# A hybrid RWKV-7/pooling decoder step: an account of array use that holds back steps of tiny products, a VectorE transpose in place of 32-wide products, and idle products in the first norm

## The chip, the cores and the metric

One NeuronCore of a Trainium2 chip runs the whole step. Its engines work side by side: TensorE (PE, with its weight loads PEld), VectorE (DVE), ScalarE (ACT), GpSimd (POOL), and the DMA queues, most of them issued from SyncE (SP). The metric is the device time of one execution in microseconds; a comparison uses medians over several runs.

## The reference

The reference is one inference step of a one-layer decoder trunk of width 1024 for a prompt of 1024 tokens and eight samples of 8 tokens, 1088 columns in all, in float32:

- `h = RMSNorm(x)`, scaled and shifted per request by a conditioning vector (the factors come from a small product with `w_ada_mix`).
- `P = h @ w_in`, 34 blocks of 128 output columns: 14 for RWKV-7, 4 for pooling, 16 for the gates.
- RWKV-7 branch: token shift, a data-dependent decay, and a recurrence over time for each of 8 heads of 64. The kernel computes it in chunks of 64 tokens, which needs the inverse of a 64x64 unit triangular matrix for each chunk, then a group norm.
- pooling branch: means over 2, 4, 8 and 16 tokens and a 128x128 product for each group.
- both branches are multiplied into the trunk through `w_br`, gated, then `w_out`, then a second norm and an MLP (`w_ff1`, squared ReLU, `w_ff2`), then a last norm.

## The kernel before

All tensors lie with features on the 128 partitions and the 1088 tokens along the free axis, in three chunks of 364, 362 and 362 (`CH`). Every large product is done as three FP32R products, high part times high, high times low, low times high (`mm3`), into PSUM.

**Order of TensorE's work.** TensorE's instructions run in the order in which they are recorded; the other engines are ordered by the framework's scheduler. `Pace.run` writes that order. It has one stream in the background (`back`: the large products of `w_in`, `w_br`, later `w_out` and the MLP; one `yield` after each three products of a chunk) and some generators in the foreground (`fore`: the chunked recurrence, pooling, norms). A foreground generator yields either a delay in modelled nanoseconds or a condition; it continues when `Pace.t`, the modelled time, has passed that delay, or the condition holds. Until then background products are recorded. `K.mm` and `K.tr` add each product's modelled duration to `Pace.t`; a change of array shape (32, 64 or 128 rows and columns) adds 200 ns. If the background yields "idle" too, `Pace.t` jumps to the earliest delay.

**Phase 1** has `start` (the first norm), then `heads` (the four head pairs f = 0 to 3 in turn), `chains` (the serial recurrence, 64x64 products), `pools` and `or_rows` in the foreground, and the `w_in` and pooling half of `w_br` products behind them. For each f, `heads` runs `front`, `scores`, then `main` (`inverse`, `level`, `affine`) beside `post` of the head pair before it; for f = 0 the neighbour is a conditioning product. `both` interleaves two such generators. Phase 2 starts with the RWKV half of `w_br` (`or_job`), which reads the result of the last `post`.

**level** finishes the triangular inverse, 32x32 blocks at a time, 16 chunks x 4 groups: a first step of 64 products, a second step of 64 products `nd` x `zd` into `ps` and 32 products `zd` x `nd` into `px` (the same blocks transposed, wanted as `x32` by the third step), then a third and a fourth step of 32 products. ACT copies `ps` into `z` with four instructions (L863), VectorE copies `px` into `x32` with two (L859). `ps` and `px` are buffers of the PSUM tag "w", which has 2; "wc" has 2 and "mm" has 4.

**rinv** (in `front` and in `post`'s `norm`) sums squares over a head with up to nine 128x128 products of 2 columns each, then ACT and VectorE make the inverse root, and `spread` transposes it back on TensorE.

**start** squares the eight blocks of x on ACT, sums them on TensorE with a matrix of ones, and then, for four groups of two feature blocks (qi = 0 to 3), computes the conditioning factors: two rounds of 32-column products (`round_`, weights `aw` by DMA), a copy to `asb` on ACT (L410), a small product `pv` (`vectors`), then the rows of h, high and low parts (`rows`, L432 to L435). The first `w_in` products run beside it as rows become ready.

## Time and profile before

| what | value |
|---|---|
| median of the three runs shown | 1767.05 us (1756.51 to 3532.46) |
| the profiled execution, whole | 1762.42 us |
| its span, first to last instruction | 1760.6 us |
| PE busy / DVE / ACT / POOL | 1702.3 / 843.5 / 549.6 / 281.9 us |
| mean granted TensorE clock over the span | 0.980 |

The page of the profile says how long each engine was busy, in which slices, at which granted clock (PEclk, in tenths), which chain of work ended last, and which groups of instructions cost most. Almost all products are recorded by the helper at L148 and are told apart by the tiles they read and write: `mm<-hx,whi` is a large product, `w<-iv,hv` and `w<-hv,iv` are the two halves of `level`'s second step, `w<-kct,wt` of 2 columns is `rinv`. One fp32 product is two instructions, one FP32R product is one.

### The profile page before, as it was taken

The numbers are of one execution on the slowest core, as the hardware profiler recorded it, in microseconds if no ns is written. First come the engines' busy times: TensorE is split into PE (matmuls) and PEld (weight loads), VectorE is DVE, ScalarE is ACT, GpSimd is POOL, SyncE is SP. The second block draws the span as 40 slices with busy tenths as digits, with TensorE's granted clock in tenths as the row PEclk, the third lists the DMA queues.
The fourth block names the chain that finished last, engine by engine and source line by source line (L and its number), as shares of the span: only waits on it lengthen the run. The fifth ranks groups of instructions, "written<-read, shape, count | busy, mean of one in ns | idle before, by whom it ended". The sixth has DMA issues, their size and how long they took to land.

```text
span 1760.6 us, 32648 instructions
## 1 busy us (share of the span) xinstructions
PE 1702.3 (97%) x13712; PEld 1590.2 (90%) x13712; DVE 843.5 (48%) x1554; ACT 549.6 (31%) x1108; POOL 281.9 (16%) x379
## 2 busy tenths in 40 slices
PE   5999999999999999999999999999999999999997
PEld 3989878887888798889889999999999999999997
DVE  5576466736583744344436633433333333333255
ACT  4443333434343433222225521313121222212132
POOL 3310101100000000004414511110111111111121
PEclk8999999989999999999999999999999999999999
DMA  9233314222413241857852321111111111111112
GB/s 335 74 124 130 124 64 136 80 82 79 162 46 128 71 139 61 292 181 258 295 176 79 125 68 43 44 47 43 48 43 43 49 43 42 48 43 43 48 43 102
DMA packets 80787, 179.61 MB, mean 102 GB/s; under 512 B 11360, under 2 KB 25696, under 8 KB 80640
## 3 DMA queue, kind: packets, MB, share of 16 engines
q1 hardware_dynamic: 72960, 155.63, 26.1%
q10 hardware_dynamic: 6048, 16.23, 2.8%
q0 software_dynamic: 1632, 5.67, 1.0%
q8 instruction: 108, 1.77, 0.4%
q14 instruction: 39, 0.32, 0.1%
HBM read 138.64 MB, written 38.84 MB: 101 GB/s over the span
## 4 chain that ended last, share of the span: by engine, by line
PE 87%; DVE 5%; DMA 3%; ACT 2%; issue 2%; POOL 1%; SPq 0%; DVEq 0%; ACTq 0%; POOLq 0%
PE mm L148 58%; PE w L148 24%; PE wc L148 4%; DMA t<-d_th 1%; PE w L155 1%; POOL t L1318 1%; DMA x<-in_xT 1%; DVE t L1377 0%; DVE wlo L168 0%; DMA hid<-in_w_ada_mlp 0%; DVE ma L1379 0%; DVE h L432 0%; DVE bk L664 0%; DVE d L496 0%; DVE t L1486 0%
## 5 line engine op out<-in xcount | busy, mean ns | idle before, releaser
L148 PE MATMUL mm<-hx,whi 128*128 128x362 f32 (+2 forms) x2608 | 683.3, 344 | 2.5 <-ACT px L517 2.0
L148 PEld LDWEIGHTS mm<-hx,whi 128*128 128x128 f32 x2608 | 459.0, 191 | 39.8 <-issue 19.2
L148 PE MATMUL mm<-hx,wlo 128*128 128x362 f32 (+3 forms) x1304 | 430.6, 330 | 0.3 <-DVE wlo L168 0.3
L167 ACT ACTIVATE whi<-wraw 128x512 fp32r<-128x512 f32 x246 | 155.1, 630 | 538.9 <-PE w L148 362.2
L148 PE MATMUL mm<-ma,whi 128*128 128x364 f32 (+1 forms) x1280 | 319.3, 330 | 0.3 <-DVE ma L1322 0.3
L148 PEld LDWEIGHTS mm<-hx,wlo 128*128 128x128 f32 x1304 | 249.8, 192 | 0.7 <-DVE wlo L168 0.6
L148 PEld LDWEIGHTS mm<-ma,whi 128*128 128x128 f32 x1280 | 227.5, 189 | 8.2 <-issue 7.5
L168 POOL TENSOR_TENSOR wlo<-wraw,whi 128x512 fp32r<-128x512 f32 x91 | 119.0, 1309 | 676.0 <-ACT whi L167 672.4
L148 PE MATMUL mm<-ma,wlo 128*128 128x364 f32 (+1 forms) x640 | 210.8, 329 | 0.2 <-DVE wlo L168 0.2
L168 DVE TENSOR_TENSOR wlo<-wraw,whi 128x512 fp32r<-128x512 f32 x155 | 108.8, 702 | 208.6 <-ACT whi L167 208.3
L1526 DVE SCALAR_TENSOR_TENSOR hx<-mm,aq,hx 128x364 f32<-128x364 f32 (+3 forms) x136 | 75.0, 588 | 206.2 <-PE mm L148 206.1
L148 PE MATMUL w<-mb,whi 128*128 128x362 f32 x576 | 143.8, 331 | 0.0
L148 PEld LDWEIGHTS mm<-ma,wlo 128*128 128x128 f32 x640 | 121.1, 189 | 0.5 <-DVE wlo L168 0.5
L1401 DVE TENSOR_TENSOR ft<-ft 128x362 f32<-128x362 f32 (+1 forms) x96 | 53.1, 576 | 131.4 <-ACT ft L1400 131.1
L148 PEld LDWEIGHTS w<-mb,whi 128*128 128x128 f32 x576 | 102.6, 191 | 2.5 <-issue 1.7
L148 PE MATMUL w<-hx,whi 128*128 128x362 f32 x416 | 103.5, 330 | 0.0
L148 PE MATMUL w<-mb,wlo 128*128 128x362 f32 x288 | 95.5, 332 | 1.8 <-DVE wlo L168 1.8
L148 PEld LDWEIGHTS w<-hx,whi 128*128 128x128 f32 x416 | 73.7, 190 | 1.7 <-issue 1.7
L148 PE MATMUL mm<-hid,whi 128*128 128x364 f32 (+4 forms) x304 | 74.9, 328 | 0.0
L1400 ACT ACTIVATE ft<-mm 128x364 f32<-128x364 f32 x64 | 29.5, 475 | 125.6 <-PE mm L148 125.5
L148 PE MATMUL w<-hx,wlo 128*128 128x362 f32 x208 | 67.8, 326 | 0.0
L1531 POOL TENSOR_TENSOR hx<-hx,rs 128x64 f32<-128x64 f32 x72 | 39.2, 544 | 142.1 <-DVE rs L1529 142.1
(330 smaller groups left out, 2196.8 us busy)
## 6 DMA issues: line engine op xcount, KB each, us to landing
wraw<-in_w_ff SPq DMA_DIRECT2D x134, 256.0 KB, 2.6
wraw<-in_w_in SPq DMA_DIRECT2D x68, 256.0 KB, 2.8
hid<-in_w_ada_mlp SPq DMA_DIRECT2D x24, 512.0 KB, 4.5
d_th<-px SPq DMA_DIRECT2D x22, 544.0 KB, 3.1
wt<-d_x SPq DMA_DIRECT2D x20, 544.0 KB, 4.3
t<-d_th ACTq DMA_DIRECT2D x16, 544.0 KB, 5.5
aw<-in_w_ada_mix SPq DMA_DIRECT2D x16, 512.0 KB, 9.2
wraw<-in_w_out SPq DMA_DIRECT2D x32, 256.0 KB, 2.7
```

The source lines that it names most:

```text
L148: return self.nc.tensor.matmul(out, lhsT, rhs, **kw)
L155: self.nc.tensor.transpose(out, in_, ident)
L167: nc.scalar.activation(hi, raw, AF.Copy)
L168: (nc.gpsimd if n < 2 or n % 2 and n >= self.solo else nc.vector).tensor_tensor(lo, raw, hi.bitcast(F32), op=ALU.subtract)
L1318: nc.gpsimd.tensor_tensor(t, t, S["u"], op=ALU.add)
L1400: nc.scalar.activation(t[:, :n], ps[:, :n], AF.Relu)
L1401: nc.vector.tensor_tensor(t[:, :n], t[:, :n], t[:, :n], op=ALU.mult)
L1526: nc.vector.scalar_tensor_tensor(x[:, c0:c0 + m], ps[:, :m], gt[:, 0:1], x[:, c0:c0 + m], op0=ALU.mult, op1=ALU.add)
L1531: nc.gpsimd.tensor_tensor(x[:, NPR:NT], x[:, NPR:NT], t, op=ALU.add)
```

## The change

`Pace` gets an account: each product adds its modelled time times a share that says how much of the array it uses (1 for FP32R, less for narrow fp32 products, 0 for fewer than 16 columns, 0.5 for transposes). `Pace.warm(t)` is a condition that a foreground step can yield in place of a delay t: the delay must have passed, and, while the background has products to give, the account over the last 3400 ns must be over `WARM` = 1700. It stands before `rinv` in `front` and in `norm`, and before all four steps of `level`; 25 times in all. When both are idle, `Pace.t` advances by 100 ns; `both` hands up one condition in place of a computed delay. In `level` the 32 products into `px` and their copies go, and VectorE transposes `ps` in 32x32 blocks into `x32`; the delay before the third step is 3000 in place of 4000. In `start`, one product of ones with x (128x128, 512 columns, never read) is put before `pv` of qi = 0, and two before the first round of qi = 1; the delays between `asb` and `pv` grow from 1100 to 1800, and to 2600 for qi = 1.

```diff
+    def spend(self, t, share):
+        self.t += t
+        self.work.append((self.t, t * share))
+
+    def warm(self, t):
+        end = self.t + t
+        def ready():
+            while self.work and self.work[0][0] < self.t - 3400:
+                self.work.pop(0)
+            return self.t >= end and (not self.dense or sum(w for _, w in self.work) > WARM)
+        return ready
...
+                self.dense = r != "idle"
                 if r == "idle" and live:
-                    self.t = max(self.t, min(r for r in live.values() if not callable(r)))
+                    self.t += 100
...
-        self.pace.t += n / 2.4 + 14 if rhs.dtype == F32R else max(n / 0.6 * min(mode) / 128, 30) + 3
+        if rhs.dtype == F32R:
+            self.pace.spend(n / 2.4 + 14, 1)
+        else:
+            self.pace.spend(max(n / 0.6 * min(mode) / 128, 30) + 3, 0 if n < 16 else max(mode) / 128 if min(mode) > 32 else 0.1)
...
-        self.pace.t += 2 * math.prod(ident.shape[1:]) / 2.4 + 3
+        self.pace.spend(2 * math.prod(ident.shape[1:]) / 2.4 + 3, 0.5)
...
+        def spin(po, n):
+            for _ in range(n):
+                self.mm(po, ones, xs[0][:, 0:512], start=True, stop=True)
...
                 ps[qi] = self.ps("wc")
+                spin(ps[qi], 2 if qi == 1 else 0)
...
             pv = self.ps("wc")
+            spin(pv, 1 if qi == 0 else 0)
...
-                yield from vectors(qi, 1100)
+                yield from vectors(qi, 2600 if qi == 1 else 1800)
...
-        yield 8000 if f else 11000
+        yield self.pace.warm(8000 if f else 11000)
...
-        yield 5500
+        yield self.pace.warm(5500)
...
-        yield 3000
-        ps, px = self.ps("w"), self.ps("w")
+        yield self.pace.warm(3000)
+        ps = self.ps("w")
...
-        for c in range(16):
-            for g in G[::2]:
-                self.mm(at(px, g, c), zd[g, c, :], nd[g, c, :], **tp(g))
-        x32 = cut32(self.hv())
-        for g in G[::2]:
-            nc.vector.tensor_copy(x32[g], cut32(px)[g])
+        x32 = self.hv()
+        nc.vector.transpose(x32, ps)
+        x32 = cut32(x32)
...
-        yield 4000
+        yield self.pace.warm(3000)
...
-        yield 3000
+        yield self.pace.warm(3000)
...
-            yield 2500 if last else 5000
+            yield self.pace.warm(2500 if last else 5000)
...
-            ready = [x for x in live if (x[1]() if callable(x[1]) else x[1] <= pace.t)]
+            now = lambda: [x for x in live if (x[1]() if callable(x[1]) else x[1] <= pace.t)]
+            ready = now()
             if not ready:
-                times = [x[1] for x in live if not callable(x[1])]
-                yield (min(times) - pace.t) if times else 500
+                yield lambda: bool(now())
...
+WARM = 1700
```

More of the change, by code (lines that the diff above doesn't have):

```diff
@@ L85, in __init__ @@
         self.t = 0.0
+        self.work = []
+        self.dense = False
+    def spend(self, t, share):
[8 more added lines that the diff above has]
+        return ready
     def run(self, back, fore=(), until=lambda: False):
```

## The prediction

> **What bounds the kernel now.** I read the page first: busy times, the slices with the granted clock, the chain that ended last.

> ```profile
> span 1760.6 us, 32648 instructions
> PE 1702.3 (97%) x13712; PEld 1590.2 (90%) x13712; DVE 843.5 (48%) x1554; ACT 549.6 (31%) x1108; POOL 281.9 (16%) x379
> PEclk8999999989999999999999999999999999999999
> PE 87%; DVE 5%; DMA 3%; ACT 2%; issue 2%; POOL 1%; SPq 0%; DVEq 0%; ACTq 0%; POOLq 0%
> ```

> TensorE is busy 97% of the span and is 87% of the chain that ended last. So every microsecond of TensorE time before the end counts, and other engines count only where TensorE waits for them. What can still go is its idle time (1760.6 − 1702.3 = 58 us), products that need not be, and time at a lower clock. The clock line has rounded digits, so I next asked for stretches cut where the clock changes (PE, PEld, DVE, ACT, POOL busy, then the granted clock).

> ```profile
> 354.34:357.75 3.41, 1.53 (x152) 1.42 (x141) 0.00 (x0) 2.17 (x4) 0.00 (x0) 1.00 0.03 6
> 576.21:579.62 3.41, 3.41 (x33) 3.12 (x32) 2.59 (x7) 2.19 (x3) 0.00 (x0) 1.00 0.00 0
> 30.07:43.73 13.66, 10.73 (x42) 7.38 (x42) 11.84 (x20) 5.26 (x9) 8.82 (x14) 0.50 1.08 349
> 245.11:248.53 3.42, 3.42 (x19) 2.82 (x18) 0.28 (x1) 1.03 (x3) 0.00 (x0) 0.50 0.09 27
> 357.75:367.99 10.24, 9.57 (x73) 9.51 (x74) 1.76 (x4) 3.72 (x7) 0.00 (x0) 0.50 0.01 2
> 422.61:429.43 6.82, 6.82 (x80) 5.43 (x80) 6.75 (x12) 1.85 (x4) 0.00 (x0) 0.50 0.14 42
> 525.01:531.83 6.82, 6.82 (x27) 6.29 (x27) 0.86 (x2) 3.09 (x6) 0.00 (x0) 0.50 0.01 2
> 542.07:545.48 3.41, 3.41 (x32) 3.35 (x25) 1.42 (x3) 2.29 (x3) 0.00 (x0) 0.50 0.28 97
> 579.62:583.03 3.41, 3.41 (x19) 3.01 (x17) 0.25 (x1) 1.35 (x3) 0.00 (x0) 0.50 0.24 77
> 692.26:699.09 6.83, 6.83 (x28) 6.83 (x28) 1.79 (x4) 2.25 (x5) 0.00 (x0) 0.50 0.02 4
> 712.74:716.15 3.41, 3.41 (x47) 3.29 (x44) 0.69 (x1) 1.04 (x2) 0.00 (x0) 0.50 0.79 257
> 866.34:869.75 3.41, 3.41 (x13) 3.41 (x13) 0.00 (x0) 0.00 (x0) 0.00 (x0) 0.50 0.88 344
> 961.91:965.32 3.41, 3.41 (x13) 3.41 (x12) 3.41 (x4) 1.54 (x3) 0.71 (x1) 0.50 0.49 154
> ```

> The lower eleven rows are all the falls before the last products: half clock, in multiples of 3.41 us. TensorE is busy 61.2 us in them (the sum of the first number after the comma), so 30.6 us are lost, and nine of the eleven lie in phase 1. The stretch before a fall may be idle in part, as 354.34 to 357.75 is with 1.53 of 3.41 us, but need not be: in 576.21 to 579.62 TensorE was busy throughout and the clock still fell, after 18 two-column products. [...]

> [...]

> The three longest falls of the heads stage follow `level`'s second step. The order of time on TensorE there, and who waited for whom:

> ```profile
> 516.24 1.29 PE L148 MATMUL w<-hv,hv 32*32 32x32 f32 x128
> 358.42 1.28 PE L148 MATMUL w<-hv,iv 32*32 32x32 f32 x40 [2.55 <-issue]
> 521.01 1.25 PE L148 MATMUL w<-iv,hv 32*32 32x32 f32 x126
> 522.12 1.17 PE L148 MATMUL w<-hv,iv 32*32 32x32 f32 x63
> 524.78 3.82 PE L148 MATMUL w<-kct,wt 128*128 128x2 f32 x18 [1.48 <-ACT z L863]
> 691.19 0.50 PE L148 MATMUL w<-hv,iv 32*32 32x32 f32 x18 [2.11 <-issue]
> 577.09 2.17 PE L148 MATMUL w<-kct,wt 128*128 128x2 f32 x18
> q8 instruction: 108, 1.77, 0.4%
> q8 instruction: 3, 0.05, 1.9%
> PE mm L148 <- DVE sq L367: 13.5, 2, 11.6
> PE w L148 <- DVE wt L1071: 3.8, 3, 2.8
> ```

> Each time 2.4 us of tiny products, then a pause inside or right behind them, then `rinv`'s 18 instructions at half clock (3.82 against 2.17 us). The pause at 522 is a wait for the ACT copies that free a "w" buffer: `ps` and `px` hold both. The two at 358 and 691 wait for nothing that the profile shows. The next two rows are the instruction queue, over the span and over 350 to 362: three packets in 12 us against one in 16.3 us on average, so I take it that the tiny products use up instructions faster than they arrive. The last two are TensorE's longest waits (total, times, longest): 11.6 us in the first norm, and 2.8, the longest of the heads stage.

> **The change part by part.**

> *The products into px.* 32 in each of 4 levels, 64 instructions each at 1.17 us: −4.7. All on TensorE, with large products queued behind, so all of it counts. Without the second "w" buffer and with 128 fewer matmul and weight-load instructions in the burst, the three pauses should go: −(2.55+1.48+2.11) = −6.1. From both sides: 0 if the first 126 instructions alone run the queue dry, −6.1 if not; behind the first step (the row at 516.24, 128 instructions in 1.29 us) no pause is seen, so I take the upper end.

> What VectorE does instead:

> ```profile
> L859 DVE COPY hv<-w x8: 679/684/690, 196.2 to 692.4; 32x512 f32<-32x512 f32 x8
> 24.20 0.71 DVE L392 STREAM_TRANSPOSE sq<-sq 128x512 f32<-128x512 f32 x1 [4.32 <-ACT sq L390]
> ```

> Eight copies of 0.68 us go, four transposes of 0.71 us come (this row reads SBUF; from PSUM no row shows one, and the copies here read PSUM in 0.68, so 0.7 to 1.4). The third step waits at least 3 us for it, which covers both ends: 0. If VectorE is behind by more than 2 us at that point, TensorE waits for the rest.

> *The account.* Behind `level`'s second step `rinv` is now held until the account has refilled. By the code's own arithmetic the 64 products count 2.1 us at a share of 0.1, so about 1.5 us of large products come between, and 3 us before each next step as before. The 23.2 us of busy half clock in the three falls would shrink to nothing (−11.6) or to one window each (−6.5). The account looks back, and the 3.41 us windows run on by themselves: 2.17 us of `rinv` can still fill most of one, as at 577. I take one window in one level of three: −9.9.

> The other five falls of the heads stage (245, 422, 542, 579, 712) hold 20.5 us, 10.2 lost. Those at 245 and 579 follow an `rinv` before which large products had run, so the condition would have held and moved nothing; 422, 542 and 712 follow waits for VectorE and ACT, which no account sees. But all order moves, and the burst rows say that a few large products more are enough. Between 0 and −10.2, with new falls possible (+1.7 each), I take −2.5, near the end that the rows support. The two falls in phase 2 stay: no step there is gated, its order is as before.

> *What the waits hold up.* A gated step blocks no engine: large products are recorded in its place, and only the foreground behind it gets later. Who would wait is the start of phase 2:

> ```profile
> 795.22 0.27 PE L155 MATMUL w<-kct,sw 128*128 128x128 f32 x1
> 804.26 0.49 PE L148 MATMUL w<-hx,whi 128*128 128x362 f32 x2
> ```

> The last foreground product is at 795.2, phase 2's first job (the first to write a "w" tile from `hx`) at about 803.3, so the foreground has some 8 us to spare. It gets shorter by the px products (1.26 us modelled) and by 4000 to 3000, for each of 4 levels: 9 us. So the gates may add 17 us, 0.7 us for each of 25, before anything is late. After delays of 3 to 11 us of mostly large products the account is usually over 1700 already, so I cost them at 0.

> *The first norm.* TensorE, ACT and VectorE in order of time, and one product of 512 columns alone:

> ```profile
> 27.13 1.03 PE L148 MATMUL wc<-sel,asb 128*128 128x9 f32 x8 [0.81 <-ACT asb L410]
> 31.25 1.93 PE L148 MATMUL wc<-aw,sT 128*32 128x512 f32 x8 [1.98 <-DMA aw<-in_w_ada_mix]
> 37.05 1.88 PE L148 MATMUL wc<-sel,asb 128*128 128x9 f32 x8 [1.76 <-ACT asb L410]
> 46.05 0.60 ACT L410 ACTIVATE asb<-wc 128x512 f32<-128x512 f32 x1 [4.07 <-PE wc L148]
> 47.29 0.75 DVE L435 SCALAR_TENSOR_TENSOR hx<-h,am,hx 128x512 fp32r<-128x512 f32 x1 [3.01 <-ACT hx L433]
> 768.11 1.02 PE L148 MATMUL w<-wt,kct 128*128 128x512 f32 x2
> ```

> Three idle products are 3.1 us. One lies where TensorE waits 0.81 for `asb`, two where it waits 1.98 for weights by DMA: 2.8 covered, +0.3. Were the cover gone, +3.1. If they keep the clock up from 30 to 43.7, the 10.7 us of busy time there lose no half; but VectorE, busy 11.84 of that stretch, sets when rows of h are ready. What it gains is the second `pv` (1.88 to 1.03) and most of its wait of 3.01 behind ACT, which waits for TensorE: −3. Ends: +3.1 and −5.4. Longer delays before `pv` let large products in ahead of it and cost nothing while rows are there. Net −2.7.

> **The sum.** −4.7 −6.1 −9.9 −2.5 −2.7 = −25.9. The profiled execution took 1762.4 us (its span and 1.8 around it): 1736.5, predicted as **1736 us**. The median shown, 1767.05, is 4.6 above the profiled execution and the fastest run 5.9 below it.

> **Rivals.**

> *The account does not hold the clock.* Windows run freely, the account only looks back. Each level keeps one fall (−6.5 in place of −9.9), the other five stay, the idle products do not hold 30 to 43.7 (+0.3): 1762.4 −4.7 −6.1 −6.5 +0.3 = 1745; with the two pauses for instructions back (+4.7), 1750. For: the busy stretch before 579. Against: 1.5 us more of large products next to each burst.

> *All falls of the heads stage go.* −4.7 −6.1 −11.6 −10.2 −2.7: 1727. For: the falls are few, the other head steps run at full clock. Against: the three behind waits for VectorE and ACT.

> *Array use does not matter, only idle time.* Then the account moves products about for nothing, and only the px products and the pauses count, with +0.3 for idle products: 1752. [...] A little chance, for the pauses may be half of the cause.

> *Slower: the foreground ends after the background.* If every gate finds the account empty it adds 1.7 us, 42 in all; less the 17 to spare, some 25 us at the end of phase 1 hold foreground products alone, mostly at half clock (4 us more). 1736 +25 +4 = 1765, 3 over before. It decides from 0.7 us a gate. Against: delays of 3 us and more before most gates.

> **How the numbers follow.** Forecast 0.52 (1728 to 1746), no hold on the clock 0.22 (1743 to 1752), all falls gone 0.14 (1718 to 1728), idle time alone 0.06 (1750 to 1757), slower 0.06 (1765 and up). From 1718 to 1754 leaves out the last, most of the fourth and a little of the third: about 0.1. A change of 2%, 35 us, is about what a measurement here can tell from none; it lies at 1731.7 from the median. The third case and a third of the forecast are beyond it: faster 0.30. Slower by 2% would need 37 us more than the slower case prices: 0.03. Same 0.67.

> **What would show it.** Right: no `w<-hv,iv` group from the removed step, no pause behind `w<-iv,hv`, `rinv` at 2.2 us there; half clock in phase 1 down from 58 us to about 25; 30 to 44 at full clock; the last foreground product still before phase 2's first job. Wrong: falls as many as before at other places; a wait for the new transpose in the third step; idle TensorE near 800.

## The result and the profile after

| | before | after |
|---|---|---|
| median | 1758.50 us (11 runs) | 1750.62 us (11 runs, 1746.01 to 1757.72) |
| ratio | | 0.9953, 95% interval 0.9933 to 0.9973 |
| profiled execution | 1762.42 us | 1746.01 us |

The change gains 8 us by the medians. The forecast was 26, so the sign was right and the size was not. (Before has one run of 3532 us, which is left out of the ratio.)

The page of the changed kernel: busy times, granted clock by slices, and the chain that ended last.

```profile
span 1744.2 us, 32136 instructions
PE 1686.4 (97%) x13462; PEld 1573.4 (90%) x13462; DVE 845.4 (48%) x1550; ACT 550.8 (32%) x1108; POOL 282.3 (16%) x379
PEclk9999999998999999999999999999999999999999
PE 87%; DVE 6%; DMA 3%; ACT 2%; issue 1%; POOL 1%; SPq 0%; ACTq 0%; DVEq 0%; POOLq 0%
```

250 product instructions went, each with its weight load (128 fp32 products are 256 instructions; the three idle products are 6 more). TensorE is still the bound. Idle time was 1760.6 − 1702.3 = 58.3 us and is 1744.2 − 1686.4 = 57.8: it did not shrink. That is the first thing to read here, for 6.1 us of it should have gone.

Now the same stretches as in the prediction, cut where the clock changes (length, then PE, PEld, DVE, ACT, POOL busy, then the granted clock). A stretch at half clock is called a fall; the first row is no fall, but the place of the longest fall of before.

```profile
30.07:43.73 13.66, 11.62 (x75) 8.38 (x76) 11.85 (x20) 6.49 (x11) 7.63 (x13) 1.00 1.08 348
252.96:256.37 3.41, 3.41 (x18) 2.89 (x17) 3.38 (x7) 0.10 (x1) 0.00 (x0) 0.50 0.45 167
351.95:355.36 3.41, 3.41 (x55) 3.35 (x49) 0.69 (x1) 2.58 (x6) 0.00 (x0) 0.50 0.32 87
396.32:403.15 6.83, 6.83 (x32) 6.24 (x32) 1.52 (x6) 6.11 (x11) 0.00 (x0) 0.50 0.00 0
427.04:430.45 3.41, 3.41 (x19) 3.01 (x19) 1.37 (x3) 1.94 (x4) 0.00 (x0) 0.50 0.59 220
519.20:526.03 6.83, 6.83 (x80) 6.26 (x80) 1.46 (x3) 3.56 (x8) 0.00 (x0) 0.50 0.26 91
843.47:850.30 6.83, 4.93 (x13) 1.12 (x12) 0.73 (x2) 1.40 (x2) 1.26 (x1) 0.50 0.97 372
945.87:949.28 3.41, 3.41 (x13) 3.41 (x12) 3.41 (x5) 2.02 (x3) 0.25 (x1) 0.50 0.50 154
```

Seven falls in place of eleven, 32.2 us of busy time at half clock in place of 61.2. The stretch from 30 to 43.7 is at full clock, as forecast. Two falls still follow `level`'s second step (352, 519).

To see the parts apart I cut the span at two marks that every kernel has: the first product of the first `level` step, and phase 2's first job. The middle piece is called the heads stage below. One row of each kernel, before and then after:

```profile
189.45:804.26 614.81, 593.66 (x6897) 524.61 (x6897) 332.13 (x647) 224.39 (x481) 34.82 (x64) 0.96 0.35 116
```

```profile
183.00:783.31 600.31, 579.86 (x6641) 511.73 (x6641) 330.94 (x643) 225.12 (x481) 34.43 (x63) 0.98 0.35 119
```

Idle time is the length less the first busy time: 21.2 and 20.5. TensorE's waits in this stage (total, times, longest), of before and then of after:

```profile
PE w L148 <- issue: 4.7, 2, 2.6
PE w L148 <- ACT z L863: 1.5, 1, 1.5
PE wc L148 <- DVE S L950: 0.5, 2, 0.3
```

```profile
PE wc L170 <- DVE S L976: 4.3, 4, 2.8
PE mm L170 <- ACT px L564: 1.6, 1, 1.6
PE w L170 <- issue: 1.3, 1, 1.3
```

The waits on `issue`, which I take for pauses for instructions, did shrink, 4.7 to 1.3. (The 1.3 stands at 513.8. Another profile of the changed kernel, after_third below, puts the same wait down to VectorE's copy L594, and here that copy ends 0.1 us before the wait does, so it is likely no pause for instructions at all.) In their place the serial recurrence (`chains`, tile S) waits 4.3 for VectorE. Where that comes from, on TensorE and VectorE of the changed kernel:

```profile
425.78 0.33 PE L170 MATMUL wc<-S,ra 64*64 64x64 f32 x4 [2.79 <-DVE S L976]
```

```profile
416.62 0.45 DVE L679 TENSOR_SCALAR wt<-wt 128x576 f32<-128x576 f32 x1
417.78 1.35 DVE L680 TENSOR_TENSOR_SCAN wt<-kscan,wt 128x576 f32<-128x576 bf16 x1
...
424.66 0.75 DVE L693 SCALAR_TENSOR_TENSOR bk<-wt,wt 64x576 f32<-64x576 f32 x1
425.44 0.28 DVE L976 SCALAR_TENSOR_TENSOR S<-S,end,wc 128x64 f32<-128x64 f32 x1
```

The small update of S stands in VectorE's queue behind the next head pair's `front` (L679 to L693), which keeps VectorE busy without a gap; TensorE waits, and a fall (427) follows.

### The profile page after: what moved, and what is told of

It is laid out like the page before. It is cut to its first block, busy times and chain, and to the rows that moved or that the text cites. A ratio compares the mean times of both kernels' runs of the same rounds, so it can differ in the third digit from the quotient of the medians.

```text
span 1744.2 us, 32136 instructions
## 1 busy us (share of the span) xinstructions
PE 1686.4 (97%) x13462; PEld 1573.4 (90%) x13462; DVE 845.4 (48%) x1550; ACT 550.8 (32%) x1108; POOL 282.3 (16%) x379
## 4 chain that ended last, share of the span: by engine, by line
PE 87%; DVE 6%; DMA 3%; ACT 2%; issue 1%; POOL 1%; SPq 0%; ACTq 0%; DVEq 0%; POOLq 0%
PE mm L170 58%; PE w L170 23%; PE wc L170 4%; DMA t<-d_th 2%; PE w L177 1%; POOL t L1344 1%; DMA x<-in_xT 1%; DVE t L1403 0%; DMA hid<-in_w_ada_mlp 0%; DVE ma L1405 0%; DVE mb L1348 0%; DVE wt L680 0%; DVE wlo L190 0%; DVE h L461 0%; DVE acc L1383 0%
```

## The experiments

All were compared with the kernel before on the same chip. Heads stage, idle, and busy at half clock are of one profiled execution each, cut as above (the last is the busy time in all stretches of the stage at clock 0.50); profiles of one kernel differ by up to 4.4 us in the stage, as the three of the full change show. No kernel here leaves out work.

| kernel | median us | ratio, interval | heads stage | idle | at half |
|---|---|---|---|---|---|
| before_again | 1759.38 | 0.9994 (0.9979 to 1.0010) | 613.3 | 20.5 | 41.0 |
| px_only | 1751.34 | 0.9951 (0.9934 to 0.9968) | 600.1 | 21.7 | 19.1 |
| account_only | 1752.65 | 0.9953 (0.9935 to 0.9971) | 599.6 | 17.4 | 17.1 |
| norm_only | 1758.97 | 0.9986 (0.9974 to 0.9999) | 612.9 | 21.4 | 40.7 |
| after_again | 1749.30 | 0.9937 (0.9920 to 0.9954) | 602.0 | 21.5 | 23.7 |
| after_third | 1750.41 | 0.9931 (0.9908 to 0.9953) | 604.8 | 23.0 | 27.1 |
| no_account | 1743.98 | 0.9912 (0.9892 to 0.9931) | 600.4 | 19.0 | 25.6 |
| px_norm | 1745.82 | 0.9914 (0.9900 to 0.9927) | 600.2 | 19.1 | 25.6 |
| px_back | 1746.08 | 0.9926 (0.9908 to 0.9945) | 601.4 | 19.3 | 17.1 |
| no_norm | 1747.71 | 0.9927 (0.9903 to 0.9951) | 600.1 | 19.6 | 23.9 |
| after_5300 | 1750.69 | 0.9948 (0.9930 to 0.9966) | 594.1 | 18.8 | 10.2 |
| act_first | 1742.83 | 0.9905 (0.9885 to 0.9925) | 596.7 | 18.5 | 19.2 |
| fill2 | 1742.14 | 0.9888 (0.9875 to 0.9902) | 599.0 | 20.7 | 19.1 |
| fill_act | 1743.35 | 0.9906 (0.9884 to 0.9927) | 596.9 | 19.8 | 16.3 |
| px_norm_4000 | 1736.10 | 0.9867 (0.9845 to 0.9889) | 590.6 | 14.4 | 13.7 |
| after_4000 | 1733.83 | 0.9858 (0.9834 to 0.9882) | 588.6 | 14.8 | 6.8 |
| before_3000 | 1764.62 | 1.0022 (1.0005 to 1.0039) | 612.8 | 24.9 | 29.9 |
| fill_4000 | 1736.45 | 0.9863 (0.9842 to 0.9885) | 593.0 | 14.3 | 20.5 |

### One part alone

The kernel before with the px edit and its shorter delay; with the account; with the first norm's edit; and unaltered.

```diff
# px_only
-        ps, px = self.ps("w"), self.ps("w")
+        ps = self.ps("w")
...
+        nc.vector.transpose(x32, ps)
...
-        yield 4000
+        yield 3000
# account_only
-        yield 3000
+        yield self.pace.warm(3000)
...
# norm_only
+                spin(ps[qi], 2 if qi == 1 else 0)
...
```

> The kernel before, unchanged, once more. Theory 'draw' (the windows of the clock gate run freely, so each execution falls at other places, and the profile of before at 1762.4 us and that of after at 1746.0 are a high and a low draw): the ratio is 1.000, the executions scatter over some 10 us, and this profile shows another set of falls in the heads stage, with 20 to 30 us lost to half clock in all where the first showed 30.6. Rival 'fixed' (falls follow from the program's order alone): the same falls at the same places within a window, 29 to 32 us lost.

> Only the level step: the 32 products into px and their copies go, the transpose by VectorE comes, the delay before the third step is 3000. Theory 'as summed': 4.7 us of products and 6 us of pauses behind them go, and the falls behind the second step get shorter: 1745 to 1750 against 1758.5. Rival 'idle moves' (what TensorE does not wait for there it waits for a few us later, for ACT and VectorE): only the 4.7 us, 1753 to 1755, with idle time of TensorE in the heads stage as before, 25 us, and the three falls still there.

> Only the first norm: three idle products and the longer delays before pv. Theory 'as summed': 30 to 44 us at full clock, the first level begins 3 us earlier, 1755 to 1756. Rival 'paid for': the idle products cost their 3.1 us and win little, since VectorE sets when rows of h are ready: 1757 to 1759, the first level no earlier than 188. Third possibility, larger: the 10.7 us at half clock count in full, the first level 5 to 6 us earlier, 1753.

> Only the account and its 25 waits; the px products stay, the first norm is as before. Theory 'as summed': the falls behind the second step of level shrink to about one window, 10 to 12 us less lost, 1746 to 1749. Rival 'looks back' (the windows run freely and the account does not look ahead, so falls only move): half-clock busy time in the heads stage stays at about 45 us or more, 1755 to 1760. The pauses stay in both, since px stays.

The px edit alone and the account alone each bring the heads stage from 613 or 615 to 600, and the full change brings it to 600 to 605: they do not add. Both break up the same burst, the one by removing a third of it, the other by putting large products behind it; that the falls which one takes are then not there for the other is the likely reason.

px_only also bears on what the clock goes by: idle time stayed (21.7) and busy time at half clock went from 41 or 44 to 19. But its pauses moved away from the bursts, and it has the shorter delay too, so this sum does not part idle time from array use. The single falls show one thing more, that the clock fell without idle time too. In the twenty profiles 107 falls begin between 180 and 810 us. 38 of them come right behind a stretch of 3.41 us in which TensorE's record has no idle time (351.9 in the changed kernel is one); in all 38 this stretch holds 14 to 18 of `rinv`'s two-column instructions, in ten of them 32x32 products too. The emptiest stretch ahead of any of the 107 still holds 0.61 us of work.

The norm is worth 2 us by the medians, with an interval that nearly reaches 1; in the profiles the piece ahead of the heads stage takes 183.6 with it, and 189.5 and 185.1 in the two of before.

### One part taken out, and repeats

no_account is the full change with `WARM = -1` (the condition always holds); px_norm is the px edit and the norm's written into the kernel before, which gives TensorE the same order; no_norm leaves out the idle products and keeps 1100; px_back puts the px products and the 4000 back.

```diff
# no_account
-WARM = 1700
+WARM = -1
# px_back
-        x32 = self.hv()
-        nc.vector.transpose(x32, ps)
...
+                self.mm(at(px, g, c), zd[g, c, :], nd[g, c, :], **tp(g))
...
-        yield self.pace.warm(3000)
+        yield self.pace.warm(4000)
```

> The changed kernel, unchanged, once more. Theory 'draw': the first profile of it (1746.0) was a low execution of its eleven, 1746 to 1758; ratio 0.995 again, and this profile shows other falls in the first norm and in phase 2, while the stretch from the first level to phase 2 is 600 us within 2 and has the same 2.8 us wait for S by the chain. Rival: the falls of the heads stage are drawn as well, and that stretch differs by more than 4 us.

> The changed kernel with WARM at -1: every gate lets its step through as soon as its delay has passed; the transpose and the idle products stay. Theory 'overlap' (the transpose alone takes away the burst that the account was to space out): no slower than the change, 1748 to 1752, the stretch from the first level to phase 2 at 600. Rival 'adds up' (the account brought 8 us alone, so it brings them here too): 1757 to 1760.

> The changed kernel without the idle products and with the delay of 1100 before pv, so the transpose and the account alone. Theory: the first norm is a stage of its own, so its part comes off as it came alone, 2 to 3 us: 1752.5 to 1754. Rival 'larger': by the first level's start (183 to 184 us with it, 185 to 190 without) it is worth 4 to 5: 1755 to 1756.

> The kernel before with the px edit and the first norm's edit, no account at all. TensorE's order of work is the one of no_account, so this is a second measurement of it beside the full change on the same chip. Overlap theory (the px edit alone already takes the heads stage from 614 to 600 us, the account adds nothing): ratio 0.991 to 0.994, 1744 to 1749 us, heads stage about 600, the first norm at full clock, no slower than the full change. Rival (no_account was a lucky draw and the account is worth some 3 us beside px): 0.996, 1753 us, slower than the full change beside it.

> The full change with the 32 products into px and VectorE's copies back, and the delay of 4000 before the third step: account and first norm without the px edit. Overlap theory: heads stage about 600 us as in account_only, less 4 us in the first norm: ratio 0.993 to 0.995, 1748 to 1752 us. Rival (the edits add, px is worth 7 us of its own): 0.9975, 1756 us, heads stage 607.

> The full change unaltered, a third time, beside px_norm on the same chip. Overlap theory: 1748 to 1752 us, 0.993 to 0.996, level with px_norm or up to 4 us slower. Rival (the account pays): 2 us or more faster than px_norm.

With any one of the three parts out, the kernel is no slower than with all. Without the account it was 5.3 and 4.6 us faster than the full change on the two chips where both ran (intervals that overlap by 0.001 and 0.002), and the heads stage is the same 600: beside the px edit the account gains nothing. In the traces TensorE's order differs from px_norm's at three places only, around `level`'s second step (346 to 365, 511 to 524 and 671 to 689 us of the changed kernel), where some large products, `rinv` and what follows it change places; elsewhere the order is the same, so the other gates found their condition met. That the account then costs some microseconds is likely, not shown. no_norm was expected to be 2 us or more slower than the full change and is level with it (1747.7 and 1749.3 on one chip), so beside the other parts the first norm's shows no gain in the time either.

px_norm also shows the px edit's own wait. ACT, VectorE and TensorE in order of time:

```profile
513.08 2.39 ACT L867 ACTIVATE z<-w 32x512 f32<-32x512 f32 x4 [2.77 <-DVE hv L862]
```

```profile
512.34 0.71 DVE L862 STREAM_TRANSPOSE hv<-w 128x512 f32<-128x512 f32 x1
```

```profile
509.69 1.29 PE L148 MATMUL w<-iv,hv 32*32 32x32 f32 x128
510.90 2.17 PE L148 MATMUL w<-kct,wt 128*128 128x2 f32 x18
515.52 1.58 PE L148 MATMUL w<-px,plw 128*128 128x364 f32 x2 [2.45 <-ACT z L867]
```

The burst ends at 511.0, VectorE reaches the transpose 1.4 us later, and ACT's copies of the same tile begin only when it has ended. So the "w" buffer, which I had freed by dropping `px`, is held longer, and the pause of 1.48 became one of 2.45. (px_only and no_account have this wait too. In the full change TensorE waits for none of these copies: there the account has changed the order behind the burst, yet idle time in the stage is no less, 20.5 to 23.0 against 19.1.) act_first tests this by putting the copies ahead of the transpose:

```diff
-        x32 = self.hv()
-        nc.vector.transpose(x32, ps)
-        x32 = cut32(x32)
         for os in HB:
...
                 nc.scalar.activation(z[rq, :16, 32 * b:32 * b + 32], cut32(ps)[rq], AF.Copy)
+        x32 = self.hv()
+        nc.vector.transpose(x32, ps)
+        x32 = cut32(x32)
```

> px_norm with ACT's four copies into z ahead of VectorE's transpose in level; all else, TensorE's order too, is the same. Theory (the px edit's new wait is ACT behind the transpose): ACT's copies start within 0.1 us of the second step's end in place of 1.4 us and more behind it, TensorE's wait of 2.4 us for z near 515 falls to about 1, idle time in the heads stage falls from 19 by 1 to 2 us, and a fall near 514 goes: ratio 0.989 to 0.991, 1743 us. Rival (that wait is a small part, the windows decide): 0.9915 as px_norm, and the third step now waits for the transpose.

ACT, TensorE and VectorE of act_first at the same place:

```profile
508.27 2.39 ACT L864 ACTIVATE z<-w 32x512 f32<-32x512 f32 x4 [0.70 <-PE w L148]
```

```profile
512.31 1.58 PE L148 MATMUL w<-px,plw 128*128 128x364 f32 x2 [1.98 <-ACT rh L315]
```

```profile
510.69 0.72 DVE L866 STREAM_TRANSPOSE hv<-w 128x512 f32<-128x512 f32 x1 [1.28 <-ACT z L864]
```

Now VectorE waits for ACT, yet TensorE still waits 1.98, and idle time fell by 0.6 only. The fall stayed (at 511 here, at 514 in px_norm). The order is real but a small part; the time, 0.9905 against 0.9914, tells nothing.

### The delay ahead of the third step

One constant of the change was left: 4000 became 3000. after_5300 raised it in the full change, to see if the chain's wait goes; the later three settle it.

```diff
# after_5300, after_4000 (the full change)
-        yield self.pace.warm(3000)
+        yield self.pace.warm(5300)      and 4000
# px_norm_4000 (px_norm)
-        yield 3000
+        yield 4000
# before_3000 (the kernel before)
-        yield 4000
+        yield 3000
```

> The changed kernel with 5300 in place of 3000 before level's third step, which gives the foreground back the modelled time that the px products and the cut from 4000 to 3000 took out of it. Theory 'alignment' (with the shorter foreground the chain's steps meet the VectorE block of front, and TensorE waits for S): the wait for S falls from 4.3 us to under 1, the stretch from the first level to phase 2 from 600 to 595, 1745 to 1747. Rival 'slack': the delay only makes the foreground later, the wait for S stays or is replaced by another, 1750 to 1753.

> px_norm with the delay of 4000 before level's third step given back. Theory (the shorter foreground brings a chain step into front's VectorE work): the wait of 2.8 us for S near 424 is back at 0.5 or less and the fall behind it goes, heads stage 597 us in place of 600. Rival (any new order meets some such wait): S gone or not, other waits of about the same sum come, heads stage 599 to 602, ratio 0.991 to 0.993.

> The full change with the delay before level's third step given back, 4000 for 3000, account and first norm as in the change. Theory (the cut delay ate the pauses' gain): heads stage 588 to 594 us, idle there 14 to 17 us, ratio 0.987 to 0.989, 1736 to 1740 us. Rival (px_norm_4000 is one lucky order, the account moves it again): heads stage 597 to 602, 0.992 to 0.994.

> The kernel before with that one delay cut from 4000 to 3000 and nothing else. Theory (a short delay brings a chain step into VectorE's block wherever it is used): slower by 3 to 8 us, ratio 1.002 to 1.005, with a wait of 2 us or more for S or for z. Rival (the cut hurts only the order of the px edit, or any reorder gives +-5): 0.995 to 1.000.

With 4000 the change gives 0.9858 in place of 0.9931 to 0.9953, 13 to 17 us faster, and without the account 0.9867 in place of 0.9914, 8 us faster. Heads stage, first of px_norm, then of after_4000:

```profile
183.35:783.56 600.21, 581.11 (x6642) 512.34 (x6641) 330.99 (x643) 225.16 (x481) 34.42 (x63) 0.98 0.35 119
```

```profile
183.32:771.93 588.61, 573.77 (x6642) 505.56 (x6641) 330.11 (x643) 223.54 (x482) 35.58 (x63) 0.99 0.36 121
```

The waits in the heads stage of before_3000, where nothing but the delay differs from before, and then of after_4000:

```profile
PE wc L148 <- DVE S L950: 4.3, 4, 2.8
PE w L148 <- ACT z L863: 3.0, 2, 1.5
PE mm L148 <- ACT px L517: 2.9, 3, 1.8
```

```profile
PE wc L170 <- DVE S L976: 2.2, 3, 1.2
PE w L177 <- ACT z L910: 2.1, 3, 0.7
```

The short delay brings the chain's wait of 4.3 (longest 2.8) into the kernel before, where it was 0.5, and the kernel is slower by 0.22%, 4 us. Where these 4 us lie its profile does not show: its heads stage (612.8) is no longer than before's, with some 4 us more idle time and 11 to 14 us less busy time at half clock. Given back in the full change, the long wait goes and the pauses for instructions do not return. The chain's wait is only 2 us of what goes (4.3 to 2.2); waits of 1.6 for ACT's copy of px (L564), 1.9 for VectorE's `wt` (L1097) and about 1 for `px` (L1297) are gone or smaller as well. How 1 us ahead of one step sets the chain against a later `front` I have argued (a shorter foreground records the next `front` earlier, while the chain keeps its own pace) and not traced: the delay changes the recorded order of thousands of rows from there on. Why the cut costs 8 us beside the px edit, 13 and more in the full change and 4 in the kernel before stays open. In the profiles the idle time makes 4.7 (px_norm) and 6.8 (the full change, mean of three) of it, and half clock 6.0 and 9.0.

More is not better: with 5300 the gain is gone. Its heads stage is shorter than the full change's (594.1), but phase 2 up to `ff2` takes 345.4 in place of 336, with 16.0 us idle (4.2 of it for the `hid` transfer), and one fall lasts 17.1 us from 836 on. The last foreground product stands at 773.2 and phase 2's first job at 776.3, so the foreground still ends before the background, if only by 3 us. That it ends too late for the first steps of phase 2 is a guess; no run here tests it.

### Idle products in phase 2

Every profile but one has a fall between 830 and 870, of 3 to 10 us (17 in after_5300), where TensorE waits for the `hid` transfer. Three idle products before that wait, in px_norm, in act_first and in px_norm_4000:

```diff
+            if name == "w_ada_mlp" and g == 0 and k2 == 1:
+                po = self.ps("wc")
+                for _ in range(3):
+                    self.mm(po, self.kc("ident"), self.kct[:, 0:512], start=True, stop=True)
```

> px_norm with three idle products of 128x512 (identity by a weight tile, never read) in phase 2, ahead of the w_ada_mlp products that wait for the hid transfer. If the falls of 3 to 10 us that every profile shows between 840 and 870 come from that wait, they go: 3 to 5 us of loss saved, 0 to 2.6 us for the products, the stage from phase 2 to ff2 at 330 to 333 us in place of 334 to 339, ratio 0.990, 1742 us. Rival (the windows are drawn freely, the fall stays or moves): the products cost up to 2.6 us and win nothing, 0.993 to 0.995, 1748 to 1751 us.

> fill2 with act_first's edit. If the two gains add: ratio 0.987, 1739 to 1741 us. If not, as fill2: 0.989, 1742 us.

> px_norm_4000 with fill2's three idle products in phase 2. If the gains add: ratio 0.984 to 0.986, 1732 to 1735 us, no fall longer than 3.4 us between 820 and 850. If the idle products win nothing, as in fill_act: 0.987, 1736 to 1738 us.

Once 3.7 us faster than its neighbour on the same chip (0.9888 against 0.9914), twice level (0.9906 and 0.9905 on the same chip, 0.9863 and 0.9867). The stage from phase 2 to `ff2` took 332.9, 337.7 and 337.1 us, against 335.6, 335.0 and 335.6 without: no gain is shown. The fall became shorter (3.4 us in all three, in place of 10.2, 6.8 and 10.2), but 3.4 is also what several profiles without these products have. The profile with no fall there is no_norm's, and its stage took 330.0.

## Why the prediction was wrong, by its own steps

Sum by stage, from the means of two profiles of before (1762.4, 1762.7) and three of the full change (1746.0, 1749.8, 1748.7):

| term | forecast | full change | after_4000 |
|---|---|---|---|
| heads stage, work at full clock | −4.7 | −3.8 | −1.7 |
| heads stage, idle ("the three pauses should go") | −6.1 | +0.8 | −6.0 |
| heads stage, half clock (half of the busy time in it) | −12.4 | −8.7 | −17.7 |
| up to the heads stage (first norm) | −2.7 | −4.2 | −4.0 |
| phase 2 and the rest | 0 | +1.5 | +0.6 |
| sum | −25.9 | −14.4 | −28.8 |

**The failed step** is the one on the shorter delay. The prediction wrote "The third step waits at least 3 us for it, which covers both ends: 0", and counted 4000 to 3000 only as 1 us a level that the foreground gains. I asked who waits for the transpose, and not what the earlier steps meet on VectorE. That cut took back the whole idle term and a part of the clock's: with the 4000 the change measures 0.9858 (0.9834 to 0.9882), and the forecast, 1736.5 of 1762.4, is 0.9853. That these two are so close is partly luck: by terms, half clock gave 5.3 more than forecast and the work 3.0 less, and the account, forecast at −9.9, is not shown to have given any of it. In my list of waits the chain's had no place, for its row in before was 0.5.

**The pauses.** The part on instructions was right (4.7 to 1.3 at most, and no row of them among after_4000's waits). What the profile has of the cause supports it: in both pauses of before a packet of 16 KB is on its way in the instruction queue q8, from 355.5 for 1.39 us (the pause is 355.9 to 358.4) and from 688.6 for 1.24 (689.1 to 691.2). That the packet ends the pause is not shown: TensorE goes on 1.6 and 1.4 us after it has landed. The part on the "w" buffer was wrong where VectorE is late: without the account, ACT's copies wait for the transpose, and TensorE for them (2.4 in px_norm).

**The account.** I put −9.9 on it. The size is near what account_only shows (half clock 42 to 17 us of busy time, so −12.6), but the px edit alone does nearly as much (−11.6), and the two do not add; I summed over one set of falls as if only the account could take them. So this term was mis-sized as well: beside the px edit and the delay of 3000 the kernel measured 5 us faster without the account. At 4000, after_4000 and px_norm_4000 lie within each other's interval, so there too the account is not shown to gain. That the clock goes by how much of the array works, on which I built the account, was my estimate, and no run shows it; the runs show 38 falls behind stretches without idle time, and 17.1 us of busy time at half clock with the account alone, against 41.0 and 43.7 in the two profiles of before.

**The first norm.** −2.7 forecast, −4 in the profiles, 2 by norm_only's median. The idle products took 3.1 us as forecast, and the stretch from 30 to 43.7 ran at full clock. The twenty profiles show that this is not luck: none of the 14 with idle products has a fall between 25 and 45 us, and all six without have one there, of 6.8 or 13.7 us. The row of the idle products:

```profile
L170 PE MATMUL wc<-x,ones 128*128 128x512 f32 x6 | 3.1, 624 | 0.0
```

**The transpose.** 0.72 us from PSUM, at the lower end of 0.7 to 1.4:

```profile
L884 DVE STREAM_TRANSPOSE hv<-w x4: 707/718/718, 188.7 to 672.2; 128x512 f32<-128x512 f32 x4
```

**The rivals.** The measured 1750.6 is the number that "the account does not hold the clock" gives with two pauses back, but not for its reason: the pauses for instructions did not come back, and half clock behind the second step fell with or without an account. "Only idle time matters" is refuted by the falls behind stretches without idle time (38 of 107). "All falls go" did not come, for five stayed in the heads stage, and "slower" did not: the last foreground product stands at 769.8, phase 2's first job at 783.3. Nor does a stretch of 3.41 us without any work lie ahead of one of the 107; the emptiest holds 0.61 us. That these 3.41 us run on by themselves, as the prediction has it, agrees with the traces: every fall but those cut by the span's end is a multiple of 3.41 us long, and in before and in the changed kernel their starts, too, lie whole multiples of it apart (from 252.96 to 351.95 it is 29, from there to 396.32 it is 13).

**The basis.** The sum was made against one profiled execution, 1762.4, which lies 1 to 4 us above the medians of before (1758.5 to 1761.5 in six comparisons), while the profiled 1746.0 of after lies 4.6 under its median. So the profiles differ by 16.4 us where the medians differ by 8 to 11. I had treated the one profile as the kernel's time.

## What to carry to other kernels

A delay in an order written out by hand is not slack to be trimmed when its own step gets shorter: it also says what the steps behind it will meet on the other engines, so price a changed constant by running it alone. Two edits that cure the same stall must not be summed; ask for each what it would still gain if the other were made first. And where profiles of one kernel differ by up to 4.4 us in one stage, as here, read a difference of a few microseconds from medians and from stages of several profiles, not from two profiles.

## What the runs showed of the hardware

```profile
L170 PE MATMUL mm<-sq,ones x18: 219/620/1222, 11.5 to 23.0; 128*128 128x512 f32 x12, 128*128 128x64 f32 x6
```

- ACT's copies of a PSUM tile began in all four levels of px_norm only after VectorE's transpose of the same tile, 0.03 us behind its end, both only reading it; in act_first, where the copies were recorded first, the transpose began 0.03 us behind the end of the last copy. Whether the chip or the framework's order asks for that wasn't tried.
